# Multiplying unit 0's x by the norm weight as it arrives, rstd applied after the matmuls, and weight conversions in row-sized packets

## The chip, the cores and the metric

The kernel runs on all 8 cores of one Trainium2 chip, two dies of four cores (0 to 3 and 4 to 7). Each core does the whole block for two of the sixteen sequences; nothing is exchanged. The metric is device time of the slowest core, in microseconds (us). Some executions of any kernel here fall into a second, slower state: the cores of one die, sometimes of both, run at a lower granted TensorE clock (one execution of the kernel before took 2944.97 us, with cores 4 to 7 at 0.81). Below, times and ratios come from fast runs alone. Where a profile fell into the slow state, only the cores whose granted clock stayed above 0.99 are used, and their number is given.

Engines: PE is TensorE, DVE VectorE, ACT ScalarE, POOL GpSimd, SP SyncE. SP issues the hardware DMA queue (loads of x, stores of y, saves of weights); POOL issues the software queue (weight loads, conversions).

## The reference, cut to what matters

```
x = x + 0.5 * swiglu(rmsnorm(x, ffn1_norm), w_gate1, w_up1, w_down1)
x = x + mixer_and_attention(rmsnorm(x, mix_norm)) @ w_out
x = x + 0.5 * swiglu(rmsnorm(x, ffn2_norm), w_gate2, w_up2, w_down2)

rmsnorm(x, g) = x * rsqrt(mean(x*x) + 1e-6) * g
swiglu(h)     = (silu(h @ w_gate) * (h @ w_up)) @ w_down
```

D_MODEL is 1024 (8 chunks of 128 partitions), D_FF 2816 (22 tiles of 128), 16 sequences of 2048 tokens. Because rstd, the rsqrt factor, is one number per token, `(x * g * rstd) @ W` equals `((x * g) @ W) * rstd`: the factor can wait until gate and up leave PSUM.

## The kernel before

A core works through eight FFN units of 1024 tokens, each in two halves (`t2`) of 512 tokens; attention work of other tokens is mixed in between. Every operation is recorded as `Op(engine, reads, writes, ...)`; a scheduler, run when the program is built, fixes the order of the instructions on each engine from modelled times. At run time an engine executes them in that fixed order.

Unit 0 starts cold. x comes as f32 in four DMAs of two chunks, each weight tile as f32 converted to bf16 on the way, into a ring of three slots. In unit 0 each tile is also saved as bf16 to a DRAM scratch, from which later units load it.

```python
def norm_ffn(u):                                  # cut: waits of other units
    for t2 in range(2):
        if u or t2 == 0:
            yield XS
            yield from x_loads(xf, s, tt, ...)    # SP: four DMAs of two chunks
        if u == 0 and t2 == 0:
            ev_first.hit()
            yield from setup()                    # SP: pvec, bfb
            yield ringA.evs[0]
            yield from x_loads(xa, s, 1, xT, False, [("rA", 0)])   # 2nd half: after weight 0
            ev_second.hit()
        r, rs_ = yield from (stats_pool() if 0 < u < 7 else stats_pe(x_, u == t2 == 0))
        for kc in range(NKC):                     # h = x * g * rstd
            yield Op("dve", x_.keys[kc] + [("rs", r), "pvec"], [("h", kc, t2)],
                     ... scalar_tensor_tensor(... in0=x_(kc), scalar=pvec[...], in1=rs_ ...))

def pair_post(u, fl, t2, bg, bu):                 # gate in bank bg, up in bank bu
    # DVE: g = copy(ps[bg]);  gu = g * ps[bu]
    # ACT: g = exp(-g); g = ln(1 + g); g = exp(-g)      -> sigmoid
    # DVE: act = g * gu

def ffn():
    order = [(fl, t2) for t2 in range(2) for fl in range(3)]     # three tiles on half 0, then on half 1
    order += [(fl, t2) for fl in range(3, NFF) for t2 in range(2)]
```

Weights of later stages are converted by DMAs from f32 DRAM to bf16 DRAM (`wd` of FFN 1 in unit 1, `wgu` of FFN 2 in unit 2, `wd` of FFN 2 in unit 3):

```python
def scratch(name, shape):
    return nc.dram_tensor(name, shape, BF16, kind="Internal").ap()
...
jobs = [(1, 4 + 2 * i, wd[0][i], wd_s[0][i], both(0, i)) for i in range(NKC)]   # (unit, step, ...)
jobs += [(1 if i < 3 else 2, 19 + i if i < 3 else i, wgu[1][i], wgu_s[1][i], ...) for i in range(NFF)]
```

## Time and profile before

| reading | before | view |
|---|---|---|
| time, median of the 3 fast ones of 4 runs | 2482.0 us | runs |
| span of the profiled core (core 6), PE busy | 2488.0 us, 2425.2 us | page, busy times |
| first gate matmul; continuous on half 1 | 20.9 us; 46.4 us | timeline |
| PE busy and granted clock in 0 to 62 us | 45.4 us, 0.89 | stretches |

The lines of the page: busy time with its share of the span and the number of instructions; the chain of waits that ended last; the DMA packets by size.

```profile
PE 2425.2 (97%) x12008; PEld 1064.3 (43%) x12008; DVE 1718.6 (69%) x2531; ACT 1392.2 (56%) x2762; POOL 573.5 (23%) x789
...
PE 83%; DMA 8%; ACT 3%; DVE 2%; issue 2%; SPq 0%; POOL 0%; DVEq 0%; ACTq 0%; POOLq 0%
```

```profile
DMA packets 122529, 384.60 MB, mean 155 GB/s; under 512 B 15088, under 2 KB 15216, under 8 KB 121456
```

PE is the limit nearly everywhere, so only its idle times and its half-clock stretches can be won. The timeline of PE at the start (start, duration, line, operation, count; in brackets the idle time before and what ended it). Tiles: `sb_xsF` and `sb_act` hold x of the two halves here, `sb_sq` its squares, `sb_hF` the normed x, `sb_wA` a gate and up weight tile, `sb_sg` gate on its way to the sigmoid, `ps` PSUM. The view ends at 62 us, which cuts its last row:

```profile
8.52 0.59 PE L567 MATMUL ps<-sb_sq,sb_ones_bf 128*128 128x512 bf16 x1 [8.52 <-ACT sb_sq L561]
...
16.22 2.40 PE L623 MATMUL ps<-sb_ones_bf 128*128 128x128 bf16 x40
20.89 1.51 PE L785 MATMUL ps<-sb_hF,sb_wA 128*128 128x512 bf16 x4 [2.28 <-DVE sb_hF L691]
23.54 8.45 PE L785 MATMUL ps<-sb_hF,sb_wA 128*128 128x512 bf16 x28 [1.14 <-DVE sb_hF L691]
34.17 0.90 PE L567 MATMUL ps<-sb_sq,sb_ones_bf 128*128 128x512 bf16 x2 [2.18 <-ACT sb_sq L561]
35.82 3.18 PE L567 MATMUL ps<-sb_sq,sb_ones_bf 128*128 128x512 bf16 x6 [0.76 <-ACT sb_sq L561]
38.80 6.01 PE L785 MATMUL ps<-sb_hF,sb_wA 128*128 128x512 bf16 x20
46.44 15.84 PE L785 MATMUL ps<-sb_hF,sb_wA 128*128 128x512 bf16 x72 [1.63 <-DVE sb_hF L691]
```

L567 are the sums of squares, L623 fillers meant to keep PE's clock up, L785 gate and up. Both halves of the tokens show the same gap: sums, rstd, eight multiplications (L691), and only then matmuls.

### The profile page before, as it was taken

Reading aid. Unit: us, or ns where it says so; the run is one execution under the profiler, and the core shown is the slowest. Engines: PE = TensorE matmul, PEld = TensorE weight load, DVE = VectorE, ACT = ScalarE, POOL = GpSimd, SP = SyncE. Lnnn points to the kernel's source line nnn. Section 1 sums busy time; section 2 is a strip of 40 time slices with the busy share of each in tenths; the row PEclk is TensorE's granted clock in tenths of the full one; section 3 lists DMA queues with packets and bytes.
Section 4 is the critical chain, followed back from the end, with each engine's and each line's share of the span. In section 5 each row is a group of like instructions: output and inputs, shape, how many; then the busy total and the mean of one; then the engine's idle time right before and its main releaser. Section 6 shows DMA issues by size and latency. Waiting matters only on the chain.

```text
span 2488.0 us, 39660 instructions; the slowest of 8 cores (2477.8 to 2488.0 us)
## 1 busy us (share of the span) xinstructions
PE 2425.2 (97%) x12008; PEld 1064.3 (43%) x12008; DVE 1718.6 (69%) x2531; ACT 1392.2 (56%) x2762; POOL 573.5 (23%) x789
## 2 busy tenths in 40 slices
PE   7999999999999899999999999999999999999999
PEld 3444444443444344443444443454434433444444
DVE  4552548965986786778857979667787799824541
ACT  4552456562785646769454576159573789603540
POOL 0114213331332331313331113422142111200000
PEclk8999999999999999999999999999999999999999
DMA  6999685668647754673656244552545531373224
GB/s 147 193 205 219 176 198 141 162 182 236 164 132 183 188 144 140 153 204 84 186 179 189 82 142 146 174 165 89 193 137 156 163 114 60 108 228 122 77 73 150
DMA packets 122529, 384.60 MB, mean 155 GB/s; under 512 B 15088, under 2 KB 15216, under 8 KB 121456
## 3 DMA queue, kind: packets, MB, share of 16 engines
q0 software_dynamic: 52624, 213.15, 34.4%
q1 hardware_dynamic: 69696, 168.90, 20.7%
q8 instruction: 101, 1.65, 0.3%
q14 instruction: 108, 0.88, 0.1%
HBM read 360.63 MB, written 91.24 MB: 182 GB/s over the span
## 4 chain that ended last, share of the span: by engine, by line
PE 83%; DMA 8%; ACT 3%; DVE 2%; issue 2%; SPq 0%; POOL 0%; DVEq 0%; ACTq 0%; POOLq 0%
PE ps L785 40%; PE ps L811 23%; PE ps L834 10%; PE ps L1026 3%; PE ps L1018 3%; PE ps L1206 2%; ACT sb_PT L1063 2%; DMA sb_wA<-wgu 2%; DMA wgu1s<-sb_wA 2%; DMA sb_xsF<-yT 1%; PE ps L567 1%; DMA wins<-sb_wM 1%; DMA sb_xsF<-xT 1%; DMA yT<-sb_xr 1%; PE ps L1123 1%
## 5 line engine op out<-in xcount | busy, mean ns | idle before, releaser
L785 PE MATMUL ps<-sb_hF,sb_wA 128*128 128x512 bf16 x5632 | 1269.5, 381 | 19.4 <-DVE sb_sg L708 7.1
L785 PEld LDWEIGHTS ps<-sb_hF,sb_wA 128*128 128x128 bf16 x5632 | 541.0, 98 | 704.6 <-issue 82.0
L811 PE MATMUL ps<-sb_act,sb_wB 128*128 128x512 bf16 x2816 | 633.4, 379 | 4.5 <-DVE sb_act L723 4.5
L1063 ACT ACTIVATE sb_PT<-ps,sb_BT 128x256 bf16<-128x256 f32 (+1 forms) x1152 | 435.5, 488 | 192.6 <-PE ps L1026 125.3
L716 ACT ACTIVATE sb_sg<-sb_sg 128x512 f32<-128x512 f32 x352 | 227.1, 645 | 453.2 <-DVE sb_sg L713 440.3
L811 PEld LDWEIGHTS ps<-sb_act,sb_wB 128*128 128x128 bf16 x2816 | 270.5, 98 | 343.2 <-issue 27.6
L713 DVE TENSOR_TENSOR sb_sg<-sb_sg,ps 128x512 f32<-128x512 f32 x352 | 240.0, 682 | 167.7 <-PE ps L785 161.2
L1091 DVE TENSOR_TENSOR sb_acc<-sb_acc,sb_PT 128x1024 f32<-128x1024 f32 (+3 forms) x288 | 323.5, 1123 | 17.8 <-POOL sb_PT L1071 8.5
L723 DVE TENSOR_TENSOR sb_act<-sb_sg 128x512 bf16<-128x512 f32 x352 | 268.1, 762 | 61.8 <-ACT sb_sg L721 60.9
L708 DVE COPY sb_sg<-ps 128x512 f32<-128x512 f32 x352 | 240.7, 684 | 69.4 <-PE ps L785 68.8
L718 ACT ACTIVATE sb_sg<-sb_sg,sb_cst 128x512 f32<-128x512 f32 x352 | 257.2, 731 | 24.4 <-ACT sb_sg L716 0.7
L721 ACT ACTIVATE sb_sg<-sb_sg 128x512 f32<-128x512 f32 x352 | 226.6, 644 | 23.0 <-ACT sb_sg L718 0.4
L755 DVE SCALAR_TENSOR_TENSOR sb_xr<-ps,sb_xr 128x512 f32<-128x512 f32 x128 | 87.5, 686 | 201.8 <-PE ps L811 189.3
L834 PE MATMUL ps<-sb_hm,sb_wM 128*128 128x512 bf16 x768 | 179.9, 382 | 5.0 <-DMA sb_wM<-wins 5.0
L592 POOL TENSOR_TENSOR sb_na<-sb_na,sb_sq 128x512 f32<-128x512 f32 x120 | 154.4, 1286 | 54.8 <-ACT sb_sq L561 49.4
L561 ACT ACTIVATE sb_sq<-sb_xsF 128x512 bf16<-128x512 f32 x184 | 115.4, 650 | 75.6 <-DMA sb_xsF<-yT 43.3
L434 POOL DMA_DIRECT2D sb_wA<-wgu2s x88 | 48.0, 545 | 424.4 <-PE ps L785 391.8
L1137 DVE RECIPROCAL sb_rs<-ps 128x128 f32<-128x128 f32 x128 | 117.6, 938 | 17.9 <-PE ps L1123 17.7
L834 PE MATMUL ps<-sb_yc,sb_wM 128*128 128x512 bf16 x512 | 122.2, 382 | 5.5 <-DMA sb_wM<-wout 4.0
L834 PEld LDWEIGHTS ps<-sb_hm,sb_wM 128*128 128x128 bf16 x768 | 75.0, 99 | 97.3 <-issue 10.1
L532 ACT ACTIVATE sb_rs<-ps,sb_cst 128x512 f32<-128x512 f32 x104 | 71.0, 688 | 78.4 <-PE ps L567 72.7
L1071 POOL TENSOR_SCALAR_AFFINE_SELECT sb_PT<-sb_PT 128x256 bf16<-128x256 bf16 x128 | 77.2, 607 | 112.9 <-ACT sb_PT L1063 112.2
(92 smaller groups left out, 1556.7 us busy)
## 6 DMA issues: line engine op xcount, KB each, us to landing
sb_xsF<-yT SPq DMA_DIRECT2D x96, 512.0 KB, 7.1
sb_wA<-wgu2s POOLq DMA_DIRECT2D x88, 512.0 KB, 3.8
sb_wA<-wgu1s POOLq DMA_DIRECT2D x66, 512.0 KB, 5.5
yT<-sb_xr SPq DMA_DIRECT2D x128, 256.0 KB, 4.0
sb_wM<-wins POOLq DMA_DIRECT2D x44, 512.0 KB, 4.1
sb_wB<-wd2s POOLq DMA_DIRECT2D x64, 352.0 KB, 4.1
sb_wB<-wd1s POOLq DMA_DIRECT2D x48, 352.0 KB, 4.6
sb_xr<-xT SPq DMA_DIRECT2D x64, 256.0 KB, 4.3
```

The source lines that it names most:

```text
L592: lambda e, a_=a_, sl=sl: e.tensor_tensor(out=na[:], in0=a_, in1=sq_t[:, tok(sl)], op=ALU.add), c_pool(TT))
L708: lambda e: e.tensor_copy(out=g, in_=ps[bg][:]), c_dve(TT))
L713: lambda e: e.tensor_tensor(out=gu, in0=g, in1=ps[bu][:], op=ALU.mult), c_dve(TT))
L716: lambda e: e.activation(out=g, in_=g, func=AF.Exp, scale=-1.0), c_act(TT, False))
L718: lambda e: e.activation(out=g, in_=g, func=AF.Ln, bias=one_t, scale=1.0),
L721: lambda e: e.activation(out=g, in_=g, func=AF.Exp, scale=-1.0), c_act(TT, False))
L723: lambda e: e.tensor_tensor(out=act_ap(fl, t2), in0=g, in1=gu, op=ALU.mult),
L785: ins = e.matmul(ps[b][:], lhsT=w[:, part * 1024 + kc * 128: part * 1024 + (kc + 1) * 128], rhs=hF[:, kc * 1024 + t2 * TT: kc * 1024 + (t2 ...
L811: ins = e.matmul(ps[b][:], lhsT=w[:, k:k + 128], rhs=act_ap(fl, t2), start=(fl == 0), stop=(fl == NFF - 1))
L834: ins = e.matmul(ps[bank][:], lhsT=w[:, off + kc * 128: off + (kc + 1) * 128], rhs=src[:, tok(kc)], start=(kc == 0), stop=(kc == NKC - 1))
L1063: lambda e, s_=s_, a=a, z=z, hq=hq, b=b, pt=pt, c=c, j=j: e.activation(out=PT[:, pt * 1024 + s_ * TT + a: pt * 1024 + s_ * TT + z], in_=ps ...
L1091: lambda e, w=w, a_=a_: e.tensor_tensor(out=a_, in0=a_, in1=w, op=ALU.add),
```

## The change

It has two independent parts. The start: chunks of unit 0's x are multiplied by the norm weight as they land, and rstd is applied at the evacuation of gate (in place of the copy) and once more to the product that contains up. Weight 0 is requested at once; the second half of x waits for weight 1. The conversions: a padded row pitch of the scratch keeps a conversion from being merged into large packets, and those of unit 1 come later.

```diff
 def scratch(name, shape):
-    return nc.dram_tensor(name, shape, BF16, kind="Internal").ap()
+    t = nc.dram_tensor(name, shape[:2] + [shape[2] + 64], BF16, kind="Internal").ap()
+    return t[:, :, 0:shape[2]]
...
-jobs = [(1, 4 + 2 * i, wd[0][i], ...
+jobs = [(1, 7 + 2 * i if i < 7 else 20, wd[0][i], ...
...
 ringA = Ring("rA", wA, 3, 2048, list(items_a()),
-             {0: (ev_first, [("xF", 1)]), 2: (ev_second, [("act", LAST + 1, 0)])})
+             {1: (ev_first, [("xF", 3)]), 2: (ev_first, [("xF", 7)])})
...
+def norm_first():
+    yield XS
+    yield from setup()
+    yield from x_loads(xf, 0, 0, xT, False)
+    ev_first.hit()
+    sc.spawn(warm(60), P_NF)                       # fillers
+    for t2, x_ in enumerate((xf, xa)):
+        if t2:
+            yield ringA.evs[1]
+            yield from x_loads(xa, 0, 1, xT, False, [("rA", 1)])
+        sc.spawn(first_stats(t2, x_), P_POST)
+        for kc in range(NKC):
+            yield Op("dve", x_.keys[kc] + ["pvec"], [("h", kc, t2)],
+                     ... tensor_scalar(... in0=x_(kc), scalar1=pvec[:, kc: kc + 1] ...))
...
 def pair_post(u, fl, t2, bg, bu):
+    # u == 0: g = ps[bg] * rstd instead of the copy
     ...
+    if u == 0:
+        yield Op("dve", [("sg", gl), ("rs", r)], [("sg", gl)],
+                 ... tensor_tensor(out=gu, in0=gu, in1=rs_, op=ALU.mult) ...)
... (cut: the first tile alternates gate and up by halves of its chunks)
```

More of the change, by code (lines that the diff above doesn't have):

```diff
@@ L496, in both @@
                 return [("wd", f, 2 * i), ("wd", f, 2 * i + 1)]
-            jobs = [(1, 4 + 2 * i, wd[0][i], wd_s[0][i], both(0, i)) for i in range(NKC)]
+            jobs = [(1, 7 + 2 * i if i < 7 else 20, wd[0][i], wd_s[0][i], both(0, i)) for i in range(NKC)]
             jobs += [(1 if i < 3 else 2, 19 + i if i < 3 else i, wgu[1][i], wgu_s[1][i], [("wgu", 1, i)])
@@ L509, in build_nc @@
         ev_act = {(u, fl, t2): Ev() for u in range(8) for fl in range(NFF) for t2 in range(2)}
-        ev_first, ev_second = Ev(), Ev()
+        ev_first = Ev()
         LAST = NFF - NKC
         ringA = Ring("rA", wA, 3, 2048, list(items_a()),
-                     {0: (ev_first, [("xF", 1)]), 2: (ev_second, [("act", LAST + 1, 0)])})
+                     {1: (ev_first, [("xF", 3)]), 2: (ev_first, [("xF", 7)])})
         ringB = Ring("rB", wB, 4, NFF * 64, list(items_b()), {i: (ev_act[(0, 7 + 2 * i, 0)], [("act", 7 + 2 * i, 0)]) for i in range(4)})
@@ L569, in ones_mm, with stats_pe @@
             SQ.put(sl)
-        def stats_pe(x_, warmup):
+        def stats_pe(x_):
             bank = yield MB
@@ L577, in stats_pe @@
                 yield from ones_mm(bank, sl, kc == 0, kc == NKC - 1)
-                if warmup:
-                    yield from warm(8 if kc < NKC - 1 else 40)
                 sl = nx
@@ L664, in fold, with first_stats @@
                     ev_cv[("win", i)].hit()
+        rs_first = {}
+        ev_rs = [Ev(), Ev()]
+        ev_xs = Ev(2)
+        used = [NFF, NFF]
+        def norm_first():
[11 more added lines that the diff above has]
+                    yield Op("dve", x_.keys[kc] + ["pvec"], [("h", kc, t2)],
+                             lambda e, kc=kc, x_=x_, t2=t2: e.tensor_scalar(
+                                 out=hF[:, kc * 1024 + t2 * TT: kc * 1024 + (t2 + 1) * TT],
+                                 in0=x_(kc), scalar1=pvec[:, kc: kc + 1], scalar2=None,
+                                 op0=ALU.mult), c_dve(TT, True))
+                ev_nf[(0, t2)].hit()
+                if t2 == 0:
+                    ev_xs.hit()
+            yield ev_xs
+            XS.put(0)
+        def first_stats(t2, x_):
+            rs_first[t2] = yield from stats_pe(x_)
+            ev_rs[t2].hit()
+            if t2 == 0:
+                ev_xs.hit()
         def norm_ffn(u):
@@ L673, in norm_ffn @@
                     yield ev_x2[(s, tt)]
-                if u:
-                    yield ev_tail[u - 1]
-                x_ = xf if u or t2 == 0 else xa
-                if u or t2 == 0:
-                    yield XS
-                    yield from x_loads(xf, s, tt, yT if f else xT, f, late=8000.0 if 0 < u < 7 else None)
-                if u == 0 and t2 == 0:
-                    ev_first.hit()
-                    yield from setup()
-                    yield ringA.evs[0]
-                    yield from x_loads(xa, s, 1, xT, False, [("rA", 0)])
-                    ev_second.hit()
-                r, rs_ = yield from (stats_pool() if 0 < u < 7 else stats_pe(x_, u == t2 == 0))
-                if u:
-                    yield ev_gate[u - 1]
+                yield ev_tail[u - 1]
+                yield XS
+                yield from x_loads(xf, s, tt, yT if f else xT, f, late=8000.0 if u < 7 else None)
+                r, rs_ = yield from (stats_pool() if u < 7 else stats_pe(xf))
+                yield ev_gate[u - 1]
                 for kc in range(NKC):
-                    yield Op("dve", x_.keys[kc] + [("rs", r), "pvec"], [("h", kc, t2)],
+                    yield Op("dve", xf.keys[kc] + [("rs", r), "pvec"], [("h", kc, t2)],
                              lambda e, kc=kc: e.scalar_tensor_tensor(
                                  out=hF[:, kc * 1024 + t2 * TT: kc * 1024 + (t2 + 1) * TT],
-                                 in0=x_(kc), scalar=pvec[:, gcol + kc: gcol + kc + 1],
+                                 in0=xf(kc), scalar=pvec[:, gcol + kc: gcol + kc + 1],
                                  in1=rs_, op0=ALU.mult, op1=ALU.mult), c_dve(TT, True))
                 RS.put(r)
-                if x_ is xf:
-                    XS.put(0)
+                XS.put(0)
                 ev_nf[(u, t2)].hit()
@@ L703, in pair_post @@
         def pair_post(u, fl, t2, bg, bu):
+            if u == 0:
+                yield ev_rs[t2]
+                r, rs_ = rs_first[t2]
             sl = yield SG
             g = sg_t[:, tok(sl)]
-            yield Op("dve", [("ps", bg)], [("sg", sl)],
-                     lambda e: e.tensor_copy(out=g, in_=ps[bg][:]), c_dve(TT))
+            if u == 0:
+                yield Op("dve", [("ps", bg), ("rs", r)], [("sg", sl)],
+                         lambda e: e.tensor_tensor(out=g, in0=ps[bg][:], in1=rs_, op=ALU.mult),
+                         c_dve(TT))
+            else:
+                yield Op("dve", [("ps", bg)], [("sg", sl)],
+                         lambda e: e.tensor_copy(out=g, in_=ps[bg][:]), c_dve(TT))
             fput(bg)
@@ L721, in pair_post @@
                      lambda e: e.activation(out=g, in_=g, func=AF.Exp, scale=-1.0), c_act(TT, False))
+            if u == 0:
+                yield Op("dve", [("sg", gl), ("rs", r)], [("sg", gl)],
+                         lambda e: e.tensor_tensor(out=gu, in0=gu, in1=rs_, op=ALU.mult), c_dve(TT))
+                used[t2] -= 1
+                if used[t2] == 0:
+                    RS.put(r)
             yield Op("dve", [("sg", sl), ("sg", gl)], [("act", fl, t2)],
@@ L779, in ffn, with mm @@
                     banks = yield from fbanks()
-                    for part in range(2):
+                    parts = [(0, 0), (0, 1), (1, 0), (1, 1)]
+                    if u == fl == 0:
+                        parts = [(0, 0), (1, 0), (0, 1), (1, 1)]
+                    for part, q in parts:
                         b = banks[part]
-                        for q in range(2):
-                            def mm(e, b=b, part=part, q=q, t2=t2, w=w):
-                                for kc in range(q * 4, q * 4 + 4):
-                                    ins = e.matmul(
-                                        ps[b][:],
-                                        lhsT=w[:, part * 1024 + kc * 128: part * 1024 + (kc + 1) * 128],
-                                        rhs=hF[:, kc * 1024 + t2 * TT: kc * 1024 + (t2 + 1) * TT],
-                                        start=(kc == 0), stop=(kc == NKC - 1))
-                                return ins
-                            yield Op("pe", [wk] + [("h", kc, t2) for kc in range(q * 4, q * 4 + 4)],
-                                     [("ps", b)], mm, c_pe(4, TT))
+                        def mm(e, b=b, part=part, q=q, t2=t2, w=w):
+                            for kc in range(q * 4, q * 4 + 4):
+                                ins = e.matmul(
+                                    ps[b][:],
+                                    lhsT=w[:, part * 1024 + kc * 128: part * 1024 + (kc + 1) * 128],
+                                    rhs=hF[:, kc * 1024 + t2 * TT: kc * 1024 + (t2 + 1) * TT],
+                                    start=(kc == 0), stop=(kc == NKC - 1))
+                            return ins
+                        yield Op("pe", [wk] + [("h", kc, t2) for kc in range(q * 4, q * 4 + 4)],
+                                 [("ps", b)], mm, c_pe(4, TT))
                     sc.spawn(pair_post(u, fl, t2, *banks), P_BANK)
@@ L1305, in norms @@
         def norms():
-            for u in range(8):
+            yield from norm_first()
+            for u in range(1, 8):
                 yield from norm_ffn(u)
```

## The prediction

> **What bounds it now.** TensorE. The busy table gives PE 2425.2 of 2488.0 us (97%); the chain of waits is 83% PE. Matmuls of 512 columns at full clock follow each other after about 0.216 us (timeline). Only some 63 us of PE idle time exist, and stretches at half clock. The stretches view: 0 to 62 us has 45.4 us busy at granted clock 0.89; no later stretch loses so much.
>
> The timeline of the start: chunks of x land from 7.6 to 13.3 us; squares, ones-matmuls and 96 fillers on PE until about 18; rstd by 17.9; eight DVE multiplications of 0.67 us until 23.4; first gate matmuls at 20.9, continuous at 23.5, the first 12 at half pace. Three weight tiles on the first half of the tokens end at 32; PE waits 2.2, does the second half's statistics, rstd, multiplications, and is continuous from 46.4. By then 52 of unit 0's 704 matmuls are done, 11.2 us of work at full pace: about 35 us lost.
>
> **What changes.** Removed: the wait for rstd before the first multiplications, twice. The first matmul needs only four chunks and weight 0, now requested at about 2 us, not 8.2; but x then shares the DMA with it, and pvec and bfb go ahead of x on the issuing queue (0.85 and 0.74 us). The second half of x waits for weight 1, before for weight 0.
>
> Added: one DVE product of 128x512 f32 per pair, 44 times 0.7 us = 31 us in unit 0. DVE was 57% busy (62 to 124 us); about 78% stays hidden behind the pair's 3.45 us on PE. The copy out of PSUM becomes a product at the same cost (0.684 against 0.682 us). The new multiplication has one tensor operand; the Trainium skill, "VectorE: DVE Perf Modes" (2x two-port mode), says fp32 tensor_scalar gets 2x and tensor_tensor does not: I expect below 0.5 us each; no run here shows it yet.
>
> **Start after, an estimate from those times:** first matmul about 11.5 us; other four chunks about 16; weight 1 about 19; weight 2 about 23; second half of x from 25 to 29; its matmuls continuous from about 29 instead of 45.5 us. First evacuations wait for rstd (about 18 us), but six PSUM banks may be in flight. Gain here about 16 us, all critical.
>
> **What may be given back.** DMA is 97 to 98% busy from 62 to 186 us, but POOL mostly waits for PE to free a weight slot (118 us, against 17 for the save), so PE sets the pace, narrowly. Before, DMA rested from about 38 to 50 us and the saves had drained; that rest disappears. I allow 2 to 4 us of PE waits on weights.
>
> **Conversions.** Only 1,073 of 122,529 packets are 8 KB or more, mostly the 38 conversions (22.5 MB). The Trainium skill, "DMA: Bandwidth & Descriptors" (Arbitration), says an engine changes queues only between packets; 4 KB packets should shorten SP's loads in units 1 to 3, but weight loads sit in the conversions' own queue and may lose share. PE's waits ended by DMA there are 5.0 us (wins) and 4.0 us (wout): worth 0 to 5 us, with the later slots.
>
> **Prediction:** 2467 us, range 2457 to 2477. Faster by over 2%: 0.01; within 2%: 0.98; slower: 0.01.
>
> **Signs.** Right: first gate matmul 10 to 13 us, second half continuous 27 to 32 us, unit 0's first down matmul at 175 to 179 us instead of 190.8, the lead kept to the end. Wrong: PE waits on sb_wA or rstd in unit 0, or stalls after 300 us that differ by over 5 us. What could break it: weight and x loads slow each other more; the fixed instruction order puts second-half multiplications, waiting for x, ahead of evacuations on DVE; a reshuffled order in later units.

## The result, and the profile after

The changed kernel took 2473.18 us (median of 4 runs, 2472.01 to 2474.24). The ratio of the fast runs is 0.9954, with a 95% interval of 0.9929 to 0.9978, so about 11 us less. A ratio is the mean time of one kernel's fast runs over that of the other's of the same rounds, so not quite the ratio of the medians quoted.

The same lines of the profile after. Line numbers moved: gate and up are L826 now, the sums L569.

```profile
PE 2402.6 (97%) x11739; PEld 1060.9 (43%) x11972; DVE 1738.0 (70%) x2575; ACT 1391.3 (56%) x2762; POOL 578.4 (23%) x789
...
PE 81%; DMA 9%; ACT 3%; issue 3%; DVE 3%; POOL 0%; SPq 0%; DVEq 0%; ACTq 0%; POOLq 0%
```

```profile
DMA packets 126529, 384.60 MB, mean 156 GB/s; under 512 B 15088, under 2 KB 15216, under 8 KB 126320
```

Some matmul records are missing from this trace (11,739 against 11,972 weight loads), so weight loads are counted below. The packets of 8 KB and more fell from 1,073 to 209. The start (core 2, again up to 62 us):

```profile
1.47 5.05 PE L623 MATMUL ps<-sb_ones_bf 128*128 128x128 bf16 x60 [1.47 <-DVE sb_cst L379]
...
16.18 2.98 PE L826 MATMUL ps<-sb_hF,sb_wA 128*128 128x512 bf16 x8
19.00 0.81 PE L569 MATMUL ps<-sb_sq,sb_ones_bf 128*128 128x512 bf16 x3
19.65 1.89 PE L826 MATMUL ps<-sb_hF,sb_wA 128*128 128x512 bf16 x8
23.24 7.07 PE L826 MATMUL ps<-sb_hF,sb_wA 128*128 128x512 bf16 x31 [1.70 <-DMA sb_wA<-wgu]
33.30 0.90 PE L569 MATMUL ps<-sb_sq,sb_ones_bf 128*128 128x512 bf16 x2 [3.00 <-ACT sb_sq L563]
34.86 0.38 PE L569 MATMUL ps<-sb_sq,sb_ones_bf 128*128 128x512 bf16 x1 [0.66 <-ACT sb_sq L563]
35.08 4.44 PE L826 MATMUL ps<-sb_hF,sb_wA 128*128 128x512 bf16 x12
...
41.30 20.88 PE L826 MATMUL ps<-sb_hF,sb_wA 128*128 128x512 bf16 x94
```

The waits for DVE's multiplications (L691) are gone. New ones stand in their place: weight 1 lands only at 23 us, and half 1 starts at 35, behind a wait for squares of the second half of x.

To see where the gain arises I read five milestones in every core's timeline (the first weight load of the stage named) and average over the cores, in us from the first instruction:

| milestone | before | after | difference |
|---|---|---|---|
| second tile of half 1, unit 0 | 47.5 | 40.9 | -6.6 |
| first down matmul of unit 0 | 188.8 | 181.6 | -7.2 |
| first down matmul of unit 1 | 474.9 | 463.8 | -11.1 |
| first down matmul of unit 2 | 844.5 | 826.8 | -17.7 |
| end | 2482.3 | 2466.3 | -16.0 |

About 7 us arise before 41 us and about 10 more in units 1 and 2; the 1.7 us lost after that lie within the spread of that stretch over all kernels (1637.5 to 1640.1 us). The profiled run of before was a long one (2489.05 us), so these differences, from one run each, come out larger than the 11 us of the timed runs; read them as places, good to a few us.

### The profile page after: what moved, and what is told of

The parts are those of the page before. It is cut to its first block, busy times and chain, and to the rows that moved or that the text cites. A ratio compares the mean times of both kernels' runs of the same rounds, so it can differ in the third digit from the quotient of the medians.

```text
span 2472.4 us, 39472 instructions; the slowest of 8 cores (2456.5 to 2472.4 us)
## 1 busy us (share of the span) xinstructions
PE 2402.6 (97%) x11739; PEld 1060.9 (43%) x11972; DVE 1738.0 (70%) x2575; ACT 1391.3 (56%) x2762; POOL 578.4 (23%) x789
## 3 DMA queue, kind: packets, MB, share of 16 engines
q1 hardware_dynamic: 69696, 168.90, 20.2%
## 4 chain that ended last, share of the span: by engine, by line
PE 81%; DMA 9%; ACT 3%; issue 3%; DVE 3%; POOL 0%; SPq 0%; DVEq 0%; ACTq 0%; POOLq 0%
PE ps L826 39%; PE ps L852 23%; PE ps L875 9%; PE ps L1067 3%; PE ps L1059 3%; DMA sb_wA<-wgu 2%; PE ps L1247 2%; DMA wgu1s<-sb_wA 2%; ACT sb_PT L1104 2%; DMA sb_xsF<-xT 1%; PE ps L569 1%; DMA sb_wA<-wgu1s 1%; DMA yT<-sb_xr 1%; DMA wd1s<-wd 1%; PE ps L1164 1%
## 5 line engine op out<-in xcount | busy, mean ns | idle before, releaser
L826 PE MATMUL ps<-sb_hF,sb_wA 128*128 128x512 bf16 x5500 | 1252.7, 380 | 21.7 <-DMA sb_wA<-wgu 3.4
L826 PEld LDWEIGHTS ps<-sb_hF,sb_wA 128*128 128x128 bf16 x5632 | 539.9, 98 | 694.2 <-issue 68.8
L751 ACT ACTIVATE sb_sg<-sb_sg,sb_cst 128x512 f32<-128x512 f32 x352 | 257.1, 731 | 24.3 <-ACT sb_sg L749 0.7
L741 DVE COPY sb_sg<-ps 128x512 f32<-128x512 f32 x308 | 210.2, 683 | 47.9 <-PE ps L826 45.2
L592 POOL TENSOR_TENSOR sb_na<-sb_na,sb_sq 128x512 f32<-128x512 f32 x120 | 156.6, 1305 | 47.9 <-ACT sb_sq L563 42.3
```

The costliest lines, as they stand in the source:

```text
L592: lambda e, a_=a_, sl=sl: e.tensor_tensor(out=na[:], in0=a_, in1=sq_t[:, tok(sl)], op=ALU.add), c_pool(TT))
L741: lambda e: e.tensor_copy(out=g, in_=ps[bg][:]), c_dve(TT))
L751: lambda e: e.activation(out=g, in_=g, func=AF.Ln, bias=one_t, scale=1.0),
L826: ins = e.matmul(ps[b][:], lhsT=w[:, part * 1024 + kc * 128: part * 1024 + (kc + 1) * 128], rhs=hF[:, kc * 1024 + t2 * TT: kc * 1024 + (t2 ...
```

## The experiments

Theory A: two separate gains, the start (about 7 us) and the conversions (the rest), and they add. Rival B: the early start alone, which also shifts the stages of units 1 and 2 past their stalls. Within the start: does not waiting for rstd gain, or the new order of the loads? And why 7 us where 16 were expected: DMA, DVE work, the order of instructions, or the clock?

"Start" below is the second tile of half 1; "down u" the first down matmul of unit u; both mean over cores as above. All kernels gave the reference's result unless said otherwise. The experiments stem from rounds on three chips, so ratios are to the kernel before in the same rounds, while milestones are compared across rounds, mostly one profile each. The kernels whose start is that of before (before, conv_only, pad_only, slots_only) differ by 1.2 us at the start and at down 0, so smaller differences there are not read. The runs below without a ratio were executed one to three times and are read by milestones alone.

### The two parts apart

start_only: the change with the two conversion edits taken back.

```diff
-    t = nc.dram_tensor(name, shape[:2] + [shape[2] + 64], ...)
-    return t[:, :, 0:shape[2]]
+    return nc.dram_tensor(name, shape, BF16, kind="Internal").ap()
-jobs = [(1, 7 + 2 * i if i < 7 else 20, wd[0][i], ...
+jobs = [(1, 4 + 2 * i, wd[0][i], ...
```

> The change without its conversion part: scratch unpadded, conversions at their old steps. Theory A (two separate gains): mean over cores 7 to 8 us below the kernel before at unit 0's first down matmul, the same 7 to 9 us at the end, so about 2474 to 2476 us. Rival B (the early start also moves the later stalls, conversions do nothing): the whole of the gain, about 16 us at the end of the mean core.

conv_only: the kernel before with both conversion edits (the same lines the other way round).

> The kernel before with only the padded scratch and the new conversion steps. Theory A: nothing in unit 0, then 2 to 4 us by unit 1's end and 6 to 9 us by the down matmuls of unit 2, kept to the end. Rival B: within 2 us of before everywhere.

pad_only: the kernel before with the padded scratch alone.

> The kernel before with only the padded scratch (row-sized packets). If packets are the cause of the gain in units 1 and 2 (theory A1): 5 to 9 us less at unit 2's first down matmul. If the later steps are (A2): within 2 us of before.

slots_only: the kernel before with the later steps alone.

> The kernel before with only the later conversion steps in unit 1. A1 (packets): within 2 us of before by unit 2. A2 (steps): 2 to 4 us less by unit 1's end, and nothing further in unit 2, whose conversion steps did not move.

| run | ratio to before, 95% interval | start | down 0 | down 1 | down 2 | end | cores |
|---|---|---|---|---|---|---|---|
| before | 1 | 47.5 | 188.8 | 474.9 | 844.5 | 2482.3 | 8 |
| the change | 0.9954 (0.9929 to 0.9978) | 40.9 | 181.6 | 463.8 | 826.8 | 2466.3 | 8 |
| start_only | 0.9972 (0.9956 to 0.9988) | 40.4 | 182.3 | 467.3 | 835.5 | 2473.1 | 4 |
| conv_only | 0.9982 (0.9967 to 0.9998) | 47.9 | 189.3 | 472.6 | 835.8 | 2474.8 | 8 |
| pad_only | 0.9983 (0.9969 to 0.9997) | 47.1 | 189.4 | 473.2 | 837.7 | 2476.0 | 8 |
| slots_only | 0.9992 (0.9973 to 1.0011) | 48.3 | 190.0 | 472.5 | 841.0 | 2478.9 | 4 |

Theory A holds. The start alone gives 2.8 thousandths, the conversions 1.8, together 4.6: what the whole change gives. Each of these has an interval of 1.6 to 2.5 thousandths to either side, so the sum fits but is not shown to be exact. start_only's fast runs took 2481.2 to 2482.2 us, not the expected 2474 to 2476; the kernel before took 2485.9 to 2490.5 us in the same rounds. Rival B falls: without the conversion edits the later lead hardly grows (6.5 us at down 0, 9.2 at the end), and the conversions alone gain 7.5 us at the end with no earlier start.

Packets and steps are told apart best by the length of the stage from unit 2's first gate weight load to its first down weight load: 235.6 us before, 235.2 in start_only and 235.2 in slots_only, but 229.6 in pad_only, 229.1 in conv_only and 228.2 with the change. Every padded kernel stayed between 227.6 and 230.2, every unpadded one at 235 or more. So the packets gain 6 to 7 us there, whatever the steps. In the timed runs padding is worth 1.7 thousandths (4 us). The later steps show perhaps 2 us in unit 1 and 3.5 at down 2 (slots_only), but their interval holds 1: not settled. The pad also changes the address of every row of the scratch. No run separates that from the packets; that x, which does not lie in the scratch, comes sooner while loads from the scratch do not (below) speaks for the packets.

### How packets in unit 2 reach PE

Before, on core 6, PE stands still for 5.05 us in this stage and then runs at half clock (12 matmuls in 5.28 us, where full clock takes about 2.6):

```profile
827.59 1.90 PE L785 MATMUL ps<-sb_hF,sb_wA 128*128 128x512 bf16 x8
834.55 5.28 PE L785 MATMUL ps<-sb_hF,sb_wA 128*128 128x512 bf16 x12 [5.05 <-DVE sb_sg L708]
```

The wait names a DVE copy (L708), but DVE itself, just before, waited 8.11 us for the end of a sigmoid on ACT:

```profile
832.30 0.69 DVE L723 TENSOR_TENSOR sb_act<-sb_sg 128x512 bf16<-128x512 f32 x1 [8.11 <-ACT sb_sg L721]
832.91 0.95 DVE L1137 RECIPROCAL sb_rs<-ps 128x128 f32<-128x128 f32 x1
833.77 0.63 DVE L708 COPY sb_sg<-ps 128x512 f32<-128x512 f32 x1
```

ACT's timeline shows the cause:

```profile
822.85 1.15 ACT L561 ACTIVATE sb_sq<-sb_xsF 128x512 bf16<-128x512 f32 x2 [3.28 <-DMA sb_xsF<-yT]
823.90 0.61 ACT L716 ACTIVATE sb_sg<-sb_sg 128x512 f32<-128x512 f32 x1
830.23 0.63 ACT L561 ACTIVATE sb_sq<-sb_xsF 128x512 bf16<-128x512 f32 x1 [5.72 <-DMA sb_xsF<-yT]
830.77 0.70 ACT L718 ACTIVATE sb_sg<-sb_sg,sb_cst 128x512 f32<-128x512 f32 x1
831.57 0.63 ACT L721 ACTIVATE sb_sg<-sb_sg 128x512 f32<-128x512 f32 x1
```

A square of the next unit's x (L561) stands in the fixed order between the first and second step of a sigmoid (L716 and L718), and its x arrives 5.7 us late. That x comes through the hardware queue while a conversion was issued at 817.7 us on the software queue. The same place with row-sized packets alone (pad_only, core 6; two lines later in numbering):

```profile
817.28 0.61 ACT L718 ACTIVATE sb_sg<-sb_sg 128x512 f32<-128x512 f32 x1
819.04 0.63 ACT L563 ACTIVATE sb_sq<-sb_xsF 128x512 bf16<-128x512 f32 x1 [1.15 <-DMA sb_xsF<-yT]
819.58 0.70 ACT L720 ACTIVATE sb_sg<-sb_sg,sb_cst 128x512 f32<-128x512 f32 x1
```

```profile
820.61 1.89 PE L787 MATMUL ps<-sb_hF,sb_wA 128*128 128x512 bf16 x8 [1.53 <-DMA sb_wA<-wgu1s]
...
824.18 4.35 PE L787 MATMUL ps<-sb_hF,sb_wA 128*128 128x512 bf16 x19 [0.16 <-issue]
```

The wait for x is 1.15 us, the 5 us stall is gone, and a smaller one appears: PE waits 1.53 us for a weight tile, whose load shares the conversions' queue. Over eight cores, from 605 to 850 us, loads of x took 10.2 us to land instead of 11.6 in the mean, and 24.3 instead of 30.5 at worst; weight loads from the scratch of FFN 1 took 7.2 instead of 6.9; the conversions 9.4 instead of 8.8. It is not core 6 alone: in the mean of eight cores, between unit 2's first gate weight load and its first down weight load PE waited 5.9 us for that copy before and 1.8 in pad_only, but 1.1 instead of 0.2 for gate and up weights. Less DMA work is not the reason: on core 6 the software queue's packets took 49.3% of the engines' time from 605 to 850 us before, and 50.7% in pad_only.

This is what the Trainium skill's page "DMA: Bandwidth & Descriptors" says under "Queues, rings and completion order": an engine turns to another queue only when a whole packet is done. In the trace the conversions before were 864 packets of 22,528 or 32,768 bytes, with a median of 2.2 and 3.1 us each (core 6); packets of 4,096 bytes, mostly loads, took 0.16 us. That the shorter turn is the reason for the earlier x is the page's mechanism; the runs show both sides of it, not the arbitration itself, nor that a packet of the profile is a packet in the page's sense.

### What gains at the start

rs_wait: the change's loads and order, but h takes in rstd again and the added products are gone.

```diff
     sc.spawn(first_stats(t2, x_), P_POST)
+    yield ev_rs[t2]
+    r, rs_ = rs_first[t2]
     for kc in range(NKC):
-        ... tensor_scalar(... scalar1=pvec[...])
+        ... scalar_tensor_tensor(... scalar=pvec[...], in1=rs_ ...)
```

> The change's loads and order, but the multiplications wait for rstd and take it in, as before; no added DVE products. If not waiting for rstd is what gains: second half's second tile starts 4 to 6 us later than with the change (45 to 47 us, mean of cores), so most of the 7 us of unit 0 is gone. If the order of the loads gains: within 2 us of the change.

It reached the start at 51.6 us and down 0 at 192.1 us (four cores of the undisturbed die): 10.5 us later at down 0 than with the change, and 3.3 us later than the kernel before. PE waits for DVE in each half again:

```profile
22.20 12.45 PE L826 MATMUL ps<-sb_hF,sb_wA 128*128 128x512 bf16 x48 [4.51 <-DVE sb_hF L688]
...
45.64 16.56 PE L826 MATMUL ps<-sb_hF,sb_wA 128*128 128x512 bf16 x66 [4.50 <-DVE sb_hF L688]
```

So not waiting for rstd is worth about 10 us here, and the rest of the start (the order of loads, the fillers) loses about 3 of them. That was further than I expected (45 to 47 us). Weight 1 landed 0.5 us later in this run than with the change (23.4 against 22.9 us on the same cores), which swells both figures a little, and the multiplication that takes rstd in is dearer (eight in a row took 5.4 us, with the change 3.25), which swells the first. The landings point to where the 3 us go (mean of eight cores, us):

| landed | before | change | w0_late | x_after_w0 |
|---|---|---|---|---|
| x, half 0, second pair of chunks | 8.8 | 13.1 | 9.8 | 9.8 |
| x, half 0, all | 12.9 | 16.1 | 13.6 | 13.4 |
| weight 0 | 16.5 | 13.4 | 16.8 | 16.7 |
| weight 1 | 19.2 | 22.4 | 20.2 | 20.0 |
| x, half 1, all | 28.1 | 33.3 | 31.7 | 29.8 |

w0_late: weight 0 requested after the first chunks of x again.

```diff
-             {1: (ev_first, [("xF", 3)]), 2: ...
+             {0: (ev_first, [("xF", 1)]), 1: (ev_first, [("xF", 3)]), 2: ...
```

> The change with weight tile 0 requested after the first x chunks again, as before. If the early request helps: everything 3 to 4 us later in unit 0. If the DMA is simply shared, x lands by 13 us and weight 0 by 17 us, first gate matmuls about 1 us later, weight 1 and the second half of x 0 to 2 us later; unit 0 ends within 2 us of the change.

x lands 2.5 us sooner, weight 0 3.4 us later; first gate matmuls at 17.0 instead of 15.9 us, start 40.5, down 0 180.5 (the change: 40.9 and 181.6). At down 0 that is within the noise. The early request is worth nothing: weight 0 comes early at the cost of the x that it is to be multiplied with.

no_xa: the second half of x is not loaded; the first half is used twice. Its result is wrong.

```diff
-    for t2, x_ in enumerate((xf, xa)):
-        if t2:
-            yield ringA.evs[1]
-            yield from x_loads(xa, 0, 1, xT, False, [("rA", 1)])
+    for t2, x_ in enumerate((xf, xf)):
```

> The change with the second half of x in unit 0 not loaded: the first half is used twice (wrong result on purpose). Theory (the start is bound by what the DMA must bring): the second half's gate matmuls follow the first half's at about 30 us instead of 35, and unit 0's first down matmul is 6 to 9 us earlier than with the change. Rival (PE order and the added DVE work bound it): under 2 us earlier.

Start 37.1 us, down 0 177.8 (four cores): 3.8 us earlier than with the change, not 6 to 9, and not under 2. Neither side met its number. The load of half 1 is a part of the bound, but the run also has another order on PE (the statistics of both halves stand before weight 1), so it isolates less than I wanted.

### DVE's work, the order, the clock

dve_twice: the added product done twice per pair (wrong result).

```diff
+        yield Op("dve", [("sg", gl), ("rs", r)], [("sg", gl)],
+                 ... tensor_tensor(out=gu, in0=gu, in1=rs_, op=ALU.mult) ...)
```

> The change with the added DVE product done twice per pair of unit 0 (wrong result on purpose): 44 times 0.69 us = 30 us more DVE work. If the added product is hidden behind PE: unit 0's first down matmul within 1.5 us of the change (181.6 us, mean of cores). If DVE is close to setting the pace: 3 us or more later.

Down 0 at 182.4 us against 181.6, within the noise. The stretches view, 62 to 124 us, gives the busy times per engine; first the change, then the run with the doubled product, both core 2:

```profile
62.00:124.00 62.00, 61.22 (x292) 28.29 (x297) 45.14 (x70) 36.41 (x57) 8.98 (x17) 1.00 0.93 195
```

```profile
62.00:124.00 62.00, 62.00 (x304) 28.73 (x303) 56.55 (x91) 37.12 (x58) 8.97 (x17) 1.00 0.96 191
```

The third pair of numbers is DVE: 45.1 us of 62 (73%) with the change, 56.6 (91%) doubled, and PE still has no gap. The product is hidden.

fill_only: 48 filler matmuls before half 1.

```diff
+    if u == fl == 0 and t2:
+        yield from warm(48)
     if fl == 0:
         yield ev_nf[(u, t2)]
```

> The change with the 48 filler matmuls alone before the second half's first tile. If the half clock after the wait for the second half of x is the cost: second half's second tile 1.5 to 2 us earlier than with the change (39 us) and the following matmuls all at full pace. If order is the cost: no change.

The half-clock matmuls disappear from the timeline, but start is at 40.2 us and down 0 at 182.0 (six cores; two ran at a clock of 0.982), the change's own on those cores being 41.0 and 181.8. No gain is seen at down 0, but this does not clear the clock: from the first to the second tile of half 1 PE took 4.4 us instead of 6.2, so the half clock costs about 1.8 us there, while in this run half 1 of x landed 1.4 us later and its first tile began 1.0 us later (same six cores). What the clock costs in the end stays open; by this run it is some 1.8 us at most.

x_early: only the order, the second half's multiplications and squares before the third pair's evacuation. The scheduler is told that x comes soon.

```diff
-    yield from x_loads(xa, 0, 1, xT, False, [("rA", 1)])
+    yield from x_loads(xa, 0, 1, xT, False, [("rA", 1)], late=1.0)
```

> The change with only the order moved: the second half's multiplications on DVE and squares on ACT stand before the third pair's evacuation. If they were held back by the order: second tile of the second half 1 to 2 us earlier than with the change. If the landing of x alone sets it: no change.

Start 37.3 us, down 0 178.2: 3.4 us earlier than the change at down 0, more than the expected 1 to 2, although x landed no sooner (33.7 us against 33.3). The order is the only edit, so the order held PE back; x_first below, with the same order, repeats it. DVE's timeline with the change (core 2) shows all eight multiplications (L686) in one block behind the evacuation of the third pair; in x_early each pair goes as its chunks land:

```profile
30.41 0.69 DVE L746 TENSOR_TENSOR sb_sg<-sb_sg,ps 128x512 f32<-128x512 f32 x1 [1.04 <-PE ps L826]
31.02 0.68 DVE L757 TENSOR_TENSOR sb_sg<-sb_sg,sb_rs 128x512 f32<-128x512 f32 x1
31.81 0.69 DVE L762 TENSOR_TENSOR sb_act<-sb_sg 128x512 bf16<-128x512 f32 x1
32.41 3.25 DVE L686 TENSOR_SCALAR sb_hF<-sb_act,sb_pvec 128x512 bf16<-128x512 f32 x8
```

```profile
29.57 0.88 DVE L686 TENSOR_SCALAR sb_hF<-sb_act,sb_pvec 128x512 bf16<-128x512 f32 x2 [1.68 <-DMA sb_act<-xT]
31.20 0.88 DVE L686 TENSOR_SCALAR sb_hF<-sb_act,sb_pvec 128x512 bf16<-128x512 f32 x2 [0.75 <-DMA sb_act<-xT]
```

### Versions that go further

x_first: x_early, the filler, and the saves of weights 1 and 2 held until the second half of x has landed.

```diff
+    late = key in (("wgu", 0, 1), ("wgu", 0, 2))           # in the save of a weight tile
+    if late:
+        yield ev_xa                                        # hit after the loads of xa are issued
-    yield Op("sp", [(self.name, sl)], [key], ...
+    yield Op("sp", [(self.name, sl)] + ([("act", NFF - 1, 0)] if late else []), [key], ...
```

> The change with three edits at its start: second-half multiplications and squares stand earlier in the instruction order, the saves of weights 1 and 2 wait for the second half of x, 48 filler matmuls keep PE busy while it waits. Expected: second half of x landed 1 to 2 us earlier, no half-clock matmuls after it, second half's second tile 2 to 4 us earlier than the change, kept to the end: 2469 to 2471 us where the change takes 2473.

2468.56 us, ratio 0.9940 (0.9926 to 0.9955), start 38.0, down 0 178.3. Half 1 of x landed at 33.3 us as before this edit, so holding back the saves moved nothing, contrary to what I expected. All it gains is x_early's order.

x_after_w0: x_early and the held saves, weight 0 after the first chunks of x, the second half of x after weight 0; no filler.

```diff
-    yield ringA.evs[1]
-    yield from x_loads(xa, 0, 1, xT, False, [("rA", 1)])
+    yield ringA.evs[0]
+    yield from x_loads(xa, 0, 1, xT, False, [("rA", 0)], late=1.0)
```

> The change with weight 0 requested after the first chunks of x and the second half of x loaded after weight 0 (both as before the change), second-half work earlier in the order, saves of weights 1 and 2 after the second half of x; no filler. Expected: second half of x landed by 27 to 30 us instead of 33, PE nearly without a gap after the third tile, second tile of the second half at 34 to 37 us (the run with the filler: 38), so 1 to 3 us less than that run: 2465 to 2468 us. If weights and x only trade places on the DMA: the same as that run within 1 us.

2466.32 us (2462.64 to 2466.77, 5 runs), ratio 0.9918 (0.9904 to 0.9933). Start 34.3 us and down 0 175.4: 13.4 us ahead of the kernel before instead of 7.2. Half 1 of x lands at 29.8 us, and PE goes from the third tile into half 1 without a gap:

```profile
17.73 12.35 PE L830 MATMUL ps<-sb_hF,sb_wA 128*128 128x512 bf16 x48 [2.33 <-DMA sb_wA<-wgu]
29.92 1.03 PE L572 MATMUL ps<-sb_sq,sb_ones_bf 128*128 128x512 bf16 x4
30.78 1.89 PE L830 MATMUL ps<-sb_hF,sb_wA 128*128 128x512 bf16 x8
```

This version beats the kernel before. Against the change it was not timed in the same rounds; by the two ratios (0.9918 and 0.9954, whose intervals touch at 0.993) it is about 9 us faster, and the milestones lie on the same side (6.2 us at down 0). It was not taken apart further, so how much of its step beyond x_first belongs to the load order, to the weight request and to the missing filler is open.

## Why the prediction was right or wrong

The time, the range and the class held: 2473.2 us lies between 2457 and 2477, 6 us above the point. But the range was wide: any gain from 5 to 25 us would have fallen into it, and the sum hid errors that partly cancel (the start too large, the losses to weights too large, the conversions too small). So the hit owes something to luck. Three of the four signs for right failed: the first gate matmul at 10 to 13 us (15.9 measured), half 1 continuous at 27 to 32 us (41.3 on core 2), down 0 at 175 to 179 us (181.6).

- "PE bounds it; the lead is kept to the end": right. From unit 2's down matmuls to the end every kernel took 1637.5 to 1640.1 us (undisturbed cores).
- "First matmul about 11.5 us; ... weight 1 about 19; weight 2 about 23; second half of x from 25 to 29; its matmuls continuous from about 29. Gain here about 16 us": **this step failed**. Measured, mean of cores: first gate matmul 15.9 us, weight 1 at 22.4, weight 2 at 25.9, second half of x 28.5 to 33.3, gain 6.6 us. The mechanism (no wait for rstd) was right and is worth about 10 us (rs_wait, with its cheaper multiplications). I had written that x and weight 0 share the DMA, but charged too little: the second pair of chunks landed at 13.1 us instead of 8.8. Half 1 of x landed 5 us later than before (33.3 against 28.1): 1.6 of them go when weight 0 is requested late (w0_late), about 2 more when x also waits for weight 0 instead of weight 1 (x_after_w0), the rest is not isolated. I also did not count that the fixed order holds its multiplications behind an evacuation (3.4 us, x_early). The list of what could break it feared the reverse, multiplications ahead of evacuations, which turned out the better order. With other loads and order (x_after_w0) the 16 us are nearly there: 13.2 us at the same milestone.
- "31 us of DVE ... stays hidden": right, with margin: twice the product is hidden too. "Below 0.5 us each" for the new multiplication: right, 0.483 us in the trace, against 0.75 us for the old one, which read a second tensor. This agrees in direction with the Trainium skill, "VectorE: DVE Perf Modes", mode 2x two-port; a whole instruction is not twice as fast (0.483 against 0.69 us for a tensor_tensor of the same size).
- "2 to 4 us of PE waits on weights" in unit 0: too much. Up to down 0 PE waited 1.9 us for weight tiles in the mean of eight cores, before 0.9; most of it is weight 1 at the start (1.70 us on core 2), so my sign for wrong, "PE waits on sb_wA", is met. From the start milestone to down 0 nothing was given back: the lead went from 6.6 to 7.2 us.
- Conversions "worth 0 to 5 us": 1.8 thousandths in the timed runs (4.5 us), 7.5 us in the profile. The direction was right on both queues: x came sooner, and a weight in the conversions' queue came later (1.53 us of PE wait). The place was wrong. I summed only the waits of PE that a DMA ended (wins, wout); the 5.05 us in unit 2 are ended by DVE, which waits for ACT, which waits for a DMA, and the half clock after it was not counted either. My sign for a wrong step, "stalls after 300 us that differ by over 5 us", is met (6 to 7 us in unit 2's stage).

Still open: how much of unit 1's 2 to 3 us belong to the later steps and how much to the packets; and how many of the 3 us that the start gives back belong to the load order and how many to the fillers; and what the half clock costs at the start.

## What to carry to other kernels

Taking a wait off an engine's start only uncovers the next one; list the landing times of every input before and after, and charge a newly early transfer to the ones that it travels with. When a wait names an engine that was itself waiting, follow it back until a DMA or real work is found, and look at what stands in front of it in the fixed order. Two parts that touch different stages are best tested apart, by the length of each stage rather than by the total.

## What the Trainium skill lacked or had wrong

- "DMA: Bandwidth & Descriptors", "SWDGE vs HWDGE vs iDMA": it gives a packet as at most 4,096 bytes preferably. The profile here shows contiguous conversions from DRAM to DRAM as packets of 22,528 and 32,768 bytes, 2.2 and 3.1 us each; a row pitch padded by 128 bytes made them row-sized (4,000 more packets in all).
- No page that I read says that cutting conversions into rows costs the loads behind them in their own queue: in unit 2's stage PE waited 1.1 us for gate and up weights instead of 0.2 (mean of eight cores), up to 1.53 us at once on core 6.
- "TensorE: Matmul & The Clock Gate", Part 1, says to budget 13/16 of the clock when three or more cores of a die run dense matmuls. Here that is not the usual state: with PE 97% busy, the fast runs had all eight cores at a mean granted clock of 0.992 to 0.998 (one, fill_only, had two cores at 0.982). The slow state does reach the page's figure: of 34 slow runs the deepest five show 0.811 to 0.820 on one die, and 13/16 is 0.8125; the others lie between that and 0.98 on the affected dies. The page's half rate after idle time does agree: 12 matmuls in 5.28 us after 5.05 us of idle time.
